# RWKV-7 recurrence on one core: TensorE work regrouped by tiling, states kept in one tile, exponentials and y transposes in other steps

## The chip, the cores and the metric

The kernel runs on one core of a Trainium2 chip. The metric is device time in microseconds (us). A core has five engines with an instruction stream each: TensorE (PE; its weight loads are listed as PEld), VectorE (DVE), ScalarE (ACT), GpSimd (POOL) and SyncE (SP), which here only issues DMAs. TensorE writes to PSUM, eight banks of 128 partitions by 512 float32; the other operands lie in SBUF. The profile's times count from the first instruction of the program.

## The reference

One inference step of a two-layer trunk: a gated DeltaNet layer and an RWKV-7 layer, on one prompt of 1024 tokens with 16 learned meta tokens ahead of it, and on 8 samples of 8 tokens. The change is in the RWKV-7 layer alone, whose core is this:

```python
def step(S, inp):
    r_t, k_t, v_t, d_t, kk_t, b_t = inp
    S = (S * d_t[:, :, None, :]
         + jnp.einsum('bhvk,bhk->bhv', S, -kk_t)[..., None] * b_t[:, :, None, :]
         + v_t[..., None] * k_t[:, :, None, :])
    return S, jnp.einsum('bhvk,bhk->bhv', S, r_t)
```

There are 16 heads with a 64x64 state each. The outputs y are normalised per head (mean, variance, weight, bias), get the bonus `sum(r*k*r_k) * v`, are gated and projected with `w_o`; the residual sum and a last RMSNorm follow.

## The kernel before

**Tiling.** The 1104 tokens are cut into three segments of 384, 384 and 336, each into six chunks of 64. Two heads form a pair, so there are 8 pairs, and one pair with one segment is an item, `P[n]`, n = 8*s + p, 24 in all. The 8 pairs' states are tiles `S[p]` of [128, 64]: the two heads' key dimensions on the partitions.

**The wave.** `wave` runs over `tau` from -3 to 54. Item n starts at `tau` = 2n and does one chunk in each step, `ci` = tau - 2n, so three items are under way at once, at chunks that lie two apart. In a step the three items' small products stand next to each other in the same PSUM banks (`pX`, `pY`, `pS`, tag "r", three banks).

**One step**, in the order of the program:
- `wave_open` takes three banks; `step_solve` multiplies the values V (the lower half of UV) with the scores G into `pX` (called "values" below), then the state S with AR into `pX` and `pY` ("solve"); ScalarE copies `pX` to X.
- `parts[0]` of the item that comes next: its scores, AR with BK, three chunks at a time into two banks of tag "f", masked to G by VectorE (L1460 to L1468).
- `step_inner`: X with TT ("TT"); ScalarE writes the negative into the upper half of UV.
- Then, each traced behind that ScalarE instruction: `step_old` (ScalarE: the old state times its decay, `pre`); steps of `rwkv_finish` for items that are done; the third part of `rwkv_front` (`pr`, its split on ScalarE, `prh`, and GpSimd); dense filling work (`fill`); `parts[1]` (the bonus in even steps; in odd ones the transposes of v, which ScalarE copies into UV at L1489).
- `step_state`: UV with BT into `pS` (state products), UV with G into `pY` (y products); VectorE makes the new states (L1600), ScalarE copies y (L1608).
- Filling work again, `parts[2]` (BK's transposes, copied to BT by ScalarE, L1476), in odd steps the y transposes of a finished item (L1645, tag "f"), `y_stats`, `rwkv_finish` up to its power on GpSimd, the loads of a new item; in even steps `front`, the second part of `rwkv_front`, with both exponentials on ScalarE (L1276, L1277), the decays' copy `DC` on GpSimd, and AR and BK on VectorE.

So an item's front goes over two steps, its parts over the next two, its six chunks over six, and its finish over three: the power, then the newton steps on VectorE (L110 to L112), `gnm` (L1636) and the y scalings on ScalarE (L1638, four in an even step, two in the odd one behind it), the transposes with `k` and `lz` on VectorE (L1647, L1648), and last the split `yh`, `yl`.

**Filling work.** `jobs` and `more` are lists of generators with a number of pieces and a first and last `tau`; `fill(now)` runs as many pieces as are due. Until `tau` 14 it is the gate projection (`zz`), then output tiles (`zo`, `do`): six dense products a piece, two pieces a tile, at whose start the next weights are cast (L86, `whi`) and at whose end VectorE adds the tile (L1740, `zst`).

**Order.** TensorE and ScalarE run in the order of the program (`manual_schedule`). VectorE, GpSimd and SyncE are ordered by a planner at build time, which takes what is ready, earlier program text first; `high_priority` puts the state update ahead. Buffers are tags with a number: a bank of "f" (two banks) is taken again as soon as its last reader is done, and the taker waits for it.

For the first segment the samples' states are read, used and written by `rwkv_sample_read` and `rwkv_sample_write`, in the first 16 steps.

Of the kernel before, what the change touches and what calls it, by code (L numbers as in the profile page):

```python
# [35 lines left out]
class Builder:  # L36
# [1368 lines left out]
    def rwkv_front(self, p, s):  # L1405
# [3 lines left out]
        P.p, P.s, P.n = p, s, 8 * s + p  # L1409
        NB = self.NB  # L1410
# [15 lines left out]
        DC = P.DC = t(fp, [128, 14], "DC", NB + 2)  # L1426
        nc.gpsimd.tensor_copy(DC[:, 0:6].unsqueeze(2), Dp[:, 1:385].rearrange("p (c k) -> p c k", k=64)[:, :, 63:64])
        if s == 0:
            nc.gpsimd.tensor_copy(DC[:, 6:14].unsqueeze(2), Dp[:, 1:65].rearrange("p (c k) -> p c k", k=8)[:, :, 7:8])
# [24 lines left out]
        def scores(c):  # L1454

            gp = [self.ps("f", 2, "G") for h in (0, 1)]
            for u in range(3):
                for h in (0, 1):
                    q = slice(64 * h, 64 * h + 64)
                    self.mm(gp[h][:, 128 * u:128 * u + 128], flat(BK[q, c + u]), AR[q, :, c + u])  # L1460
# [33 lines left out]
        if s == 0:  # L1494
            if p:
                read = self.rwkv_sample_read(P)
                next(read)
            for g in (1, 3, 5):
                P.parts[g].append(lambda: next(read, None))
        yield P  # L1500
# [36 lines left out]
    def step_solve(self, W):  # L1537

        hs = [slice(0, 64), slice(64, 128)]
        UV = self.ring_uv(W.tau)  # L1540
        for (P, ci), q in zip(W.items, W.at):
            for h in (0, 1):
                self.mmw(W, "X", h, 64 * q, P.G[:, ci, h, 0:64], UV[:, q, h])
        for (P, ci), q in zip(W.items, W.at):
# [29 lines left out]
    def step_old(self, W):  # L1574

        for P, ci in W.items:
            if 6 * P.s + ci > 1:
                P.pre = self.t(self.ap, [128, 64], "pre", 3)
                self.act(P.pre, self.S[P.p], AF.Identity, scale=P.DC[:, ci:ci + 1])

    def step_state(self, W):
# [8 lines left out]
        for (P, ci), q in zip(W.items, W.at):  # L1590
            for h in (0, 1):
                self.mmw(W, "Y", 1 - h, 64 * q, P.G[:, ci, h, 64:128], UV[:, q, h])
        with self.tc.high_priority():
            for (P, ci), q in zip(W.items, W.at):
                c = 6 * P.s + ci
                S, DC, p = self.S[P.p], P.DC, W.pS[:, 64 * q:64 * q + 64]
                if c == 1:
                    nc.vector.tensor_scalar(S, p, DC[:, ci:ci + 1], None, op0=ALU.mult)
                elif c > 1:
                    nc.vector.scalar_tensor_tensor(S, p, DC[:, ci:ci + 1], P.pre, op0=ALU.mult, op1=ALU.add)  # L1600
# [20 lines left out]
    def rwkv_finish(self, p, s, P):  # L1621
# [15 lines left out]
        for q in range(6):  # L1637
            self.act(y(q), y(q), AF.Identity, scale=rs[:, q:q + 1], bias=nm[:, q:q + 1])  # L1638
            if q == 5 or q == 3 and P.n < 23:
                yield  # L1640
        yp = self.ps("f", 2, "yT")
# [18 lines left out]
    def rwkv_sample_read(self, P):  # L1660
# [23 lines left out]
        rs = [rp, self.ps("d", 2, "rsr")]  # L1684
# [8 lines left out]
    def rwkv_sample_write(self, p, P, BT, DC):  # L1693
# [12 lines left out]
        nc.vector.tensor_tensor(P.Sb, P.Sb, DC[:, 6:14].unsqueeze(2).broadcast_to([128, 8, 64]), op=ALU.mult)  # L1706
# [219 lines left out]
    def layer1(self, ctx, right, stay, xa, xb, x):  # L1926
# [138 lines left out]
        self.S = [t(ap, [128, 64], f"rS{p}") for p in range(8)]  # L2065
# [12 lines left out]
    def wave(self, zin, first, loaded_, stay, last, pool):  # L2078
# [23 lines left out]
        def norms(s):  # L2102
            x = self.sums_in(s)
            for _ in range(2 + s):
# [3 lines left out]
        jobs = [(gates, 32, -4.5, 14), (lambda: out(0, Z), 16, 14, 22), (lambda: out(1, DD), 16, 22, 30),  # L2108
                (lambda: out(2, Z), 16, 30, 38), (lambda: out(3, DD), 16, 38, 46), (lambda: out(4, Z, None, range(6)), 12, 46, 52), (lambda: out(4, DD, x2, (6, 7)), 4, 52.1, 52.45),
                (lambda: out(5, DD, x2), 16, 52.1, 54.5), (lambda: out(6, DD, x2), 8, 54.6, 56), (lambda: self.finish_last(x2), 1, 56, 57)]  # L2110

        more = [(lambda: norms(0), 8, 31, 37.9), (lambda: norms(1), 9, 46.3, 50.2), (lambda: x2.update(self.sums_in(2, (6, 7))) or iter(()), 1, 50.3, 51),
# [33 lines left out]

        load(0)
        front()
        for tau in range(-3, 55):
            m = (tau + 2) // 2  # L2150
            parts = P[m].parts[3 * (tau % 2):3 * (tau % 2) + 3] if 0 <= m < 24 else [[], [], []]
            items = [(P[n], tau - 2 * n) for n in range(max(0, (tau - 4) // 2), min(24, tau // 2 + 1)) if 0 <= tau - 2 * n < 6]
# [79 lines left out]
```

## Time and profile before

| what | us |
|---|---|
| median of 3 runs | 2243.75 (2238.74 to 2249.12) |
| the profiled execution | 2249.0 |
| its span, first to last instruction | 2247.3 |
| the wave's first 16 steps, a stretch of | 121 (1837 to 1958) |
| its further steps | 246 (1958 to 2204) |

In the timeline a row is a start, a duration, the engine, the line, the operation, the tiles written and read, and the shapes; for a product on TensorE the pair like 64*128 is the part of the array that it uses, rows by columns, its tiling. The duration of a product includes its way through the array, so what it costs is read from start to start. A bracket tells how long the engine had been idle and what ended that. `x12` stands for twelve such instructions in a row.

### The profile page before, as it was taken

To read this page: it belongs to the slowest core of one execution; us is meant where nothing else is said; L and a number is where in the kernel's file an instruction comes from. 1 tells how busy PE (TensorE), PEld (TensorE's weight loads), DVE (VectorE), ACT (ScalarE), POOL (GpSimd) and SP (SyncE) were. 2 spreads that over 40 slices of the span, in tenths; PEclk is the share of its full clock that TensorE was granted. 3 is DMA by queue.
4 is the path that set the end of the run, shared out by engine and by line. 5 is a ranking of instruction groups with operands and counts; after the bars stand their busy time and mean duration, and the time that the engine had idled before them with its cause. 6 is when DMAs were issued, how large, how long until landed. Compare 5 with 4: busy or idle time off the path is not lost.

```text
span 2247.3 us, 55153 instructions
## 1 busy us (share of the span) xinstructions
PE 2115.6 (94%) x20452; PEld 1935.5 (86%) x20452; DVE 1551.2 (69%) x4229; ACT 1271.5 (57%) x3641; POOL 911.7 (41%) x1253
## 2 busy tenths in 40 slices
PE   5989999999999999999998999989899999999997
PEld 5888888989898898989898999979798988888876
DVE  6777858576776858577433585676887747776755
ACT  5545546555455646555633365674756446677774
POOL 3434344443434335343423154254534344444434
PEclk9999999999999999999999999989999999999999
DMA  4333242333323233343615314645566375677764
GB/s 119 94 88 106 62 113 66 101 93 92 106 73 106 64 102 95 91 115 86 187 51 152 97 52 143 223 164 177 164 183 179 109 212 158 193 222 216 228 184 144
DMA packets 430662, 292.66 MB, mean 130 GB/s; under 512 B 147145, under 2 KB 412986, under 8 KB 430394
## 3 DMA queue, kind: packets, MB, share of 16 engines
q1 hardware_dynamic: 430394, 289.14, 44.8%
q8 instruction: 161, 2.64, 0.5%
q14 instruction: 107, 0.88, 0.1%
HBM read 197.68 MB, written 91.37 MB: 129 GB/s over the span
## 4 chain that ended last, share of the span: by engine, by line
PE 57%; DVE 16%; DMA 9%; ACT 8%; issue 4%; POOL 4%; SPq 2%; DVEq 0%; POOLq 0%; ACTq 0%
PE d L76 20%; PE dz L76 5%; PE rA L76 4%; PE dk L76 4%; PE dq L76 3%; DMA attn<-drow 3%; DVE invT L473 2%; DVE invtmp L471 2%; PE rX L80 2%; DVE cvy L435 2%; PE fG L76 1%; POOL attn L545 1%; PE zo L76 1%; PE dv L76 1%; PE do L76 1%
## 5 line engine op out<-in xcount | busy, mean ns | idle before, releaser
L90 POOL TENSOR_TENSOR wlo<-wraw,whi 128x512 fp32r<-128x512 f32 (+1 forms) x246 | 324.6, 1323 | 365.4 <-ACT whi L86 329.9
L76 PE MATMUL d<-xc,whi 128*128 128x384 f32 (+2 forms) x1006 | 283.5, 341 | 0.0
L86 ACT CAST whi<-wraw 128x512 fp32r<-128x512 f32 (+1 forms) x246 | 150.2, 613 | 128.7 <-PE dq L76 50.5
L435 DVE SCALAR_TENSOR_TENSOR cvy<-raw,cw,cvy 128x408 f32<-128x408 f32 (+2 forms) x288 | 177.2, 629 | 16.6 <-ACT cvy L62 14.8
L76 PEld LDWEIGHTS d<-xc,whi 128*128 128x128 f32 (+1 forms) x1006 | 185.5, 191 | 3.1 <-DVE X L731 0.8
L76 PE MATMUL d<-xc,wlo 128*128 128x384 f32 (+3 forms) x476 | 159.0, 342 | 1.9 <-POOL wlo L90 1.9
L76 PE MATMUL dz<-xc,whi 128*128 128x384 f32 (+1 forms) x480 | 150.4, 345 | 0.0
L76 PE MATMUL d<-xa,whi 128*128 128x384 f32 (+3 forms) x450 | 144.3, 344 | 5.5 <-ACT ev L2032 3.8
L76 PE MATMUL dv<-xc,whi 128*128 128x384 f32 (+1 forms) x480 | 146.7, 335 | 0.0
L834 POOL TENSOR_SCALAR Sb<-Sb,eglb 128x128 f32<-128x128 f32 x128 | 81.5, 653 | 87.5 <-DMA Sb<-in_state_gdn 46.2
L76 PE MATMUL dz<-xa,whi 128*128 128x384 f32 (+1 forms) x288 | 101.5, 353 | 0.0
L473 DVE TENSOR_TENSOR invT<-invT,invtmp 72x31 f32<-72x31 f32 (+15 forms) x248 | 99.0, 399 | 2.8
L76 PE MATMUL dv<-xa,whi 128*128 128x384 f32 (+1 forms) x288 | 100.1, 347 | 0.1
L471 DVE TENSOR_TENSOR invtmp<-invA,invT 72x31 f32<-72x31 f32 (+15 forms) x248 | 94.3, 380 | 7.4 <-DMA invA<-ltd 4.6
L76 PEld LDWEIGHTS d<-xc,wlo 128*128 128x128 f32 (+1 forms) x476 | 90.5, 191 | 6.1 <-issue 2.7
L76 PEld LDWEIGHTS d<-xa,whi 128*128 128x128 f32 (+1 forms) x450 | 85.3, 192 | 8.7 <-ACT ev L2032 4.1
L76 PEld LDWEIGHTS dz<-xc,whi 128*128 128x128 f32 x480 | 90.3, 194 | 0.8
L76 PEld LDWEIGHTS dv<-xc,whi 128*128 128x128 f32 x480 | 88.5, 188 | 0.5 <-issue 0.4
L62 ACT ACTIVATE o<-rA,gcol 128x128 f32<-128x128 f32 x128 | 46.6, 372 | 72.7 <-DVE S L745 72.2
L62 ACT ACTIVATE attn<-attn,gcol 128x128 f32<-128x128 f32 x144 | 46.6, 390 | 72.5 <-POOL attn L545 72.4
L76 PE MATMUL d<-xa,wlo 128*128 128x384 f32 (+3 forms) x252 | 86.1, 342 | 1.4 <-POOL wlo L90 1.4
L62 ACT ACTIVATE w<-rA,nbp 128x128 f32<-128x128 f32 x144 | 51.4, 367 | 49.5 <-PE rA L76 49.0
(522 smaller groups left out, 7030.9 us busy)
## 6 DMA issues: line engine op xcount, KB each, us to landing
wraw<-in_gdn_w_in SPq DMA_DIRECT2D x96, 256.0 KB
wraw<-in_rwkv_w_rkvz SPq DMA_DIRECT2D x80, 256.0 KB
Sb<-in_state_gdn SPq DMA_DIRECT2D x64, 256.0 KB
sldcak<-cakd SPq DMA_DIRECT2D x24, 576.0 KB
wraw<-in_rwkv_w_o SPq DMA_DIRECT2D x42, 256.0 KB
E<-drow SPq DMA_DIRECT2D x24, 384.0 KB
attn<-drow SPq DMA_DIRECT2D x24, 384.0 KB
wraw<-in_gdn_w_out SPq DMA_DIRECT2D x36, 256.0 KB
```

What stands on the lines that cost most here:

```text
L62: return self.nc.scalar.activation(out, in_, func, bias=bias, scale=scale, **kw)
L76: self.nc.tensor.matmul(out, lhsT, rhs, start=start, stop=stop)
L80: self.nc.tensor.matmul(out, lhsT, rhs, start=start, stop=True, skip_group_check=True)
L86: nc.scalar.copy(hi, x)
L90: e.tensor_tensor(lo, x, hi.bitcast(F32), op=ALU.subtract)
L435: nc.vector.scalar_tensor_tensor(y[:, 0:wd], raw[:, k:k + wd], cw[k], y[:, 0:wd], op0=ALU.mult, op1=ALU.add)
L471: nc.vector.tensor_tensor(tmp, A[:, j, j + 1:32].unsqueeze(2).broadcast_to([nb, n, m]), Tv[:, j, 0:m].unsqueeze(1).broadcast_to([nb, n, m] ...
L473: nc.vector.tensor_tensor(Tv[:, j + 1:32, 0:m], Tv[:, j + 1:32, 0:m], tmp, op=ALU.subtract)
L545: nc.gpsimd.affine_select(E6, E6, pattern=[[0, 6], [1, 128]], compare_op=ALU.is_ge, fill=NEG, base=0, channel_multiplier=-1)
L834: nc.gpsimd.tensor_scalar(Sb[:, u], Sb[:, u], self.eglb[:, hv, 4 * g + u:4 * g + u + 1], None, op0=ALU.mult)
```

## The change

TensorE's work in a step is put in another order, and some other work with it:

- The values for step tau + 1 are issued at the end of step tau, right behind the y products (`step_values`, called by `opened`).
- The scores are computed with 64 columns of weights at a time instead of 128: twice as many products, half as wide.
- Both portions of filling work, `parts[1]` and `parts[2]` stand ahead of `step_state`; before, half of the filling work and `parts[2]` stood behind it.
- The y transposes come right behind `step_inner` in odd steps, into a bank of a tag chosen by `tau` (`Q.tag`). All six y scalings of an item stand in its even step.
- The second part of a front, with the exponentials, stands in odd steps behind the y transposes; the third part follows in the same step, behind the first portion of filling work.
- The 8 states lie in one tile `Sall`. `step_old` goes. The update is an addition and a multiplication on up to three neighbouring states at once, with the decays in one tile `DCr`. A segment's wrap from pair 7 to pair 0 splits it into two.
- The output tiles' due times move by 0.6, so that a tile's first piece falls into a step's second portion and its second piece into the next step's first.
- A sample's last reading step comes at the end of the odd step (`P.tail`), with its second bank from tag "f".

```diff
-        DC = P.DC = t(fp, [128, 14], "DC", NB + 2)
-        nc.gpsimd.tensor_copy(DC[:, 0:6].unsqueeze(2), Dp[:, 1:385].rearrange("p (c k) -> p c k", k=64)[:, :, 63:64])
+        nc.gpsimd.tensor_copy(self.DCr[:, 6 * p:6 * p + 6].unsqueeze(2), Dp[:, 1:385].rearrange("p (c k) -> p c k", k=64)[:, :, 63:64])
...
-                    self.mm(gp[h][:, 128 * u:128 * u + 128], flat(BK[q, c + u]), AR[q, :, c + u])
+                    for x in (0, 1):
+                        self.mm(gp[h][64 * x:64 * x + 64, 128 * u:128 * u + 128], BK[q, c + u, x], AR[q, :, c + u])
...
-    def step_solve(self, W):
-
-        hs = [slice(0, 64), slice(64, 128)]
+    def step_values(self, W):
+
         UV = self.ring_uv(W.tau)
         for (P, ci), q in zip(W.items, W.at):
             for h in (0, 1):
                 self.mmw(W, "X", h, 64 * q, P.G[:, ci, h, 0:64], UV[:, q, h])
+
+    def step_solve(self, W):
...
-    def step_old(self, W):
-
-        for P, ci in W.items:
-            if 6 * P.s + ci > 1:
-                P.pre = self.t(self.ap, [128, 64], "pre", 3)
-                self.act(P.pre, self.S[P.p], AF.Identity, scale=P.DC[:, ci:ci + 1])
...
+        live = [(P, ci, q) for (P, ci), q in zip(W.items, W.at) if 6 * P.s + ci > 0]
...
+            for r in runs:
+                (P, ci, q), n = r[0], len(r)
+                S = self.Sall[:, P.p:P.p + n]
+                x = self.t(self.ap, [128, 3, 64], "pre", 2)[:, 0:n]
+                o = 6 * P.p + ci
+                DC = self.DCr[:, o:o + 4 * n - 3:4]
+                nc.vector.tensor_tensor(x, W.pS[:, 64 * q:64 * q + 64 * n].rearrange("p (c k) -> p c k", k=64), S, op=ALU.add)
+                nc.vector.tensor_tensor(S, x, DC.unsqueeze(2).broadcast_to([128, n, 64]), op=ALU.mult)
...
             self.act(y(q), y(q), AF.Identity, scale=rs[:, q:q + 1], bias=nm[:, q:q + 1])
-            if q == 5 or q == 3 and P.n < 23:
-                yield
-        yp = self.ps("f", 2, "yT")
+        yield
+        yp = self.ps(*P.tag, "yT")
...
-        jobs = [(gates, 32, -4.5, 14), (lambda: out(0, Z), 16, 14, 22), (lambda: out(1, DD), 16, 22, 30),
+        jobs = [(gates, 32, -4.5, 14.6), (lambda: out(0, Z), 16, 14.6, 22.6), (lambda: out(1, DD), 16, 22.6, 30.6),
...
+        def opened(tau):
+            items = [(P[n], tau - 2 * n) for n in range(max(0, (tau - 4) // 2), min(24, tau // 2 + 1)) if 0 <= tau - 2 * n < 6]
+            W = self.wave_open(items, tau) if items else None
+            if W:
+                self.step_values(W)
+            return items, W
...
             with self.tc.issue_after(ins) if W else ExitStack():
-                if W:
-                    self.step_old(W)
+                if tau % 2 and 0 <= (tau - 7) // 2 < 22:
+                    Q = P[(tau - 7) // 2]
+                    Q.tag = DD if tau < 23 else Z if 23 <= tau < 30 or 39 <= tau < 46 else ("f", 2)
+                    next(Q.done)
+                if tau % 2 and loaded and tau > -2:
+                    begun.append(loaded.pop(0))
+                    next(begun[-1])
                 if tau % 2 == 0 and 0 <= (tau - 8) // 2 < 24:
                     next(P[(tau - 8) // 2].done, None)
...
                 late = [x for x in late if not next(x, True)]
+                fill(tau + 0.5)
                 for f in begun:
                     next(f)
                 begun.clear()
-                fill(tau + 0.5)
...
                 for f in parts[1]:
                     f()
-                if W:
-                    self.step_state(W)
...
                 fill(tau + 1)
                 for f in parts[2]:
                     f()
-                if tau % 2 and 0 <= (tau - 7) // 2 < 24:
-                    next(P[(tau - 7) // 2].done, None)
+                if W:
+                    self.step_state(W)
+                late = [x for x in late if not next(x, True)]
+                if tau == 51:
+                    next(P[22].done)
+                step = opened(tau + 1)
+                if tau % 2 and 0 <= m < 24 and P[m].tail:
+                    P[m].tail()
...
                 if tau % 2:
                     load((tau + 5) // 2)
-                else:
-                    front()
```

48 lines of the change are left out of this document (27 added, 21 removed).

## The prediction

> **What bounds the kernel now.** I read the page first, then the busy time by stretch, then TensorE's timeline over one pair of recurrence steps, then ScalarE's, VectorE's and GpSimd's timelines over the same pair.
>
> ```profile
> span 2247.3 us, 55153 instructions
> ...
> PE 2115.6 (94%) x20452; PEld 1935.5 (86%) x20452; DVE 1551.2 (69%) x4229; ACT 1271.5 (57%) x3641; POOL 911.7 (41%) x1253
> ```
>
> The change touches only the recurrence, some 52 steps. Its two halves (up to chunk step 16, where the samples' states are handled too, and after) by stretch; behind its length stand the busy us of PE, PEld, DVE, ACT and POOL, the granted clock, the DMA share and GB/s:
>
> ```profile
> 1837.00:1958.00 121.00, 116.92 (x1758) 96.56 (x1758) 89.82 (x296) 76.35 (x219) 54.61 (x61) 0.99 0.65 178
> 1958.00:2204.00 246.00, 236.95 (x3871) 203.73 (x3871) 167.45 (x626) 181.35 (x546) 109.31 (x118) 1.00 0.72 214
> ```
>
> The reader sees a TensorE that is never idle (237 of 246 us), at full clock, beside a ScalarE that is 74% busy. One pair on TensorE (odd step 2048.17 to 2055.62, even step to 2062.00: 13.83 us):
>
> ```profile
> 2048.17 0.57 PE L80 MATMUL rX<-UV,G 128*64 128x64 f32 x12
> ...
> 2054.78 0.91 PE L76 MATMUL fyT<-ident,y 64*64 64x64 f32 x24 [0.18 <-ACT UV L1489]
> ...
> 2055.62 0.57 PE L80 MATMUL rX<-UV,G 128*64 128x64 f32 x12
> 2056.12 0.27 PE L80 MATMUL rX<-rS,AR 64*64 64x64 f32 x2
> ...
> 2056.63 0.94 PE L76 MATMUL fG<-AR,BK 64*128 64x128 f32 x12
> 2057.49 0.27 PE L80 MATMUL rX<-X,rTT 64*64 64x64 f32 x1
> ...
> 2057.78 0.22 PE L80 MATMUL rX<-X,rTT 64*64 64x64 f32 x1
> ...
> 2057.84 0.22 PE L80 MATMUL rX<-X,rTT 64*64 64x64 f32 x1
> ...
> 2057.99 0.45 PE L76 MATMUL zo<-yh,whi 128*128 128x384 f32 x1
> 2058.27 0.34 PE L76 MATMUL zo<-yl,whi 128*128 128x384 f32 x1
> 2058.45 0.34 PE L76 MATMUL zo<-yh,wlo 128*128 128x384 f32 x1
> ...
> 2059.32 0.34 PE L76 MATMUL fbonus<-prl,bones 128*128 128x384 f32 x1
> 2059.58 0.57 PE L80 MATMUL rS<-UV,BT 128*64 128x64 f32 x12
> 2059.98 0.52 PE L80 MATMUL rY<-UV,G 128*64 128x64 f32 x12
> 2060.43 0.44 PE L76 MATMUL zo<-yh,whi 128*128 128x384 f32 x1
> ...
> 2062.00 0.57 PE L80 MATMUL rX<-UV,G 128*64 128x64 f32 x12
> ```
>
> The tiling stands behind the operands. Inside a group a round starts 0.06 us after the last (2057.78, 2057.84); where the tiling changes it takes 0.15 (2057.84 to 2057.99), and a first dense product then holds 0.28 instead of 0.18 (2057.99, 2058.27, 2058.45). A change costs 0.09, into a dense piece 0.19. After a dense product it is the same 0.09 (2059.32 to 2059.58, 0.26 instead of 0.17).
>
> **The change, part by part.**
>
> *Regrouping.* Before, the tiling changes 8 times in an odd step and 7 in an even one; afterwards three times in each (64*64, then 128*128, then 128*64). Nine changes fewer at 0.09, and two entries of four into dense work at another 0.10: 1.0 us a pair. The y transposes also lose their 0.18 of waiting. TensorE alone would need 13.83 - 1.2 = 12.6.
>
> *Scores as 24 products of 64 columns instead of 12 of 128.* No such row exists. The solve puts 24 products of 64*64 into 0.51 us (2056.12 to 2056.63), four tiles at once, with half the moving columns; doubling the columns gives up to 1.0, and equal streaming (two row halves now, four tiles then, over the same columns) 0.75 without the change of tiling. I take 0.75, since now two tiles are at work in 0.86 (2056.63 to 2057.49) and the four do the same total. The Trainium skill speaks against it ("TensorE: Matmul & The Clock Gate", section "Wait — 56ns, not 53.3ns?"): starts never come closer than about 25 ns, and 62 ns each where hardware decode is off. By 25 ns the sum stays; by 62 ns the scores would take an estimated 1.5 us. The solve's 24 in 0.51 us disagree with both.
>
> *State update.* Three fused operations and three ScalarE products (`pre`) become two operations on 128x192. For the rest of this part ScalarE and VectorE:
>
> ```profile
> 2052.61 0.50 ACT L86 CAST prh<-pr 128x384 fp32r<-128x384 f32 x1
> ...
> 2053.65 1.07 ACT L1489 COPY UV<-fVT 64x128 f32<-64x128 f32 x4
> 2054.75 0.32 ACT L1608 COPY y<-rY 128x192 f32<-128x192 f32 x1
> 2054.96 0.48 ACT L1476 COPY BT<-fBT 128x384 f32<-128x384 f32 x1
> ...
> 2058.09 0.33 ACT L62 ACTIVATE UV<-rX 64x192 f32<-64x192 f32 x1 [1.04 <-PE rS L80]
> 2058.32 0.31 ACT L62 ACTIVATE UV<-rS 64x192 f32<-64x192 f32 x1
> 2058.66 0.83 ACT L62 ACTIVATE pre<-rS,DC 128x64 f32<-128x64 f32 x3
> ...
> 2059.80 1.43 ACT L62 ACTIVATE y<-y,gnm,grs 128x64 f32<-128x64 f32 x4
> 2061.13 0.60 ACT L86 CAST whi<-wraw 128x512 fp32r<-128x512 f32 x1
> ```
>
> ```profile
> 2049.46 0.56 DVE L1431 TENSOR_TENSOR AR<-fldrv,fDp 128x384 f32<-128x384 f32 x1 [0.35 <-DMA fldrv<-rvd]
> 2049.94 0.55 DVE L1434 TENSOR_TENSOR BK<-fld2c,fiD 128x384 f32<-128x384 f32 x1
> 2050.41 0.61 DVE L1441 SCALAR_TENSOR_TENSOR pr<-fldrv,pcol,fld2c 128x384 f32<-128x384 f32 x1
> ...
> 2054.31 0.55 DVE L1740 TENSOR_TENSOR zst<-zst,do 128x384 f32<-128x384 f32 x1 [0.85 <-PE do L76]
> ...
> 2055.77 0.61 DVE L1647 SCALAR_TENSOR_TENSOR k<-fyT,lnw,rbv 128x384 f32<-128x384 f32 x1
> 2055.94 1.32 POOL L102 TENSOR_TENSOR grs<-va,cvals 128x6 f32<-128x6 f32 x1 [0.52 <-DVE va L1631]
> 2057.90 0.17 DVE L1636 SCALAR_TENSOR_TENSOR gnm<-mv,grs 128x6 f32<-128x6 f32 x1
> 2057.98 1.01 DVE L1467 TENSOR_TENSOR G<-fG,gm 128x384 f32<-128x384 f32 x2
> 2060.28 0.67 DVE L1600 SCALAR_TENSOR_TENSOR rS<-rS,DC,pre 128x64 f32<-128x64 f32 x3
> ```
>
> ```profile
> L62 ACT ACTIVATE fDp<-fld2c 128x384 f32<-128x384 f32 x23 | 12.3, 537 | 0.0
> ...
> L1465 DVE TENSOR_TENSOR G<-fG,gms 128x128 f32<-128x128 f32 x14 | 4.0, 285 | 1.5 <-PE fG L76 1.5
> ```
>
> 128x192 lies between 0.285 (128x128) and 0.55 (128x384): 0.35 each, as a guess from those ends. ScalarE is relieved of 3 x 0.24 a step, which is worth nothing by itself. What is new is that little covers the update: it starts 0.70 after the state products (2059.58 to 2060.28), ends at 0.70 + 0.35 + 0.35, and reaches TensorE at 1.5, which by then has had the state products 0.40, the y products 0.35 and the next step's values 0.45, 1.2 in all. TensorE waits 0.3 a step with the whole next step behind it. Bound by TensorE alone, a pair takes 12.6 + 0.6 = 13.2.
>
> *Exponentials, y scaling and transposes moved; this decides.* ScalarE runs in the order of the program. In an odd step the exponentials now stand behind UV, and `prh` right behind them; `prh` needs `pr`, hence AR and BK, hence the exponentials. Before, half a step lay between. Let T be the first product with TT, 1.16 after the solve (0.41 + 0.75). UV starts T+0.60 and ends T+1.14 (2057.49, 2058.09, 2058.63); two exponentials at 0.54, overlapping by 0.1, end at T+2.1. VectorE gets k at T+1.3 (24 transposes behind the TT products) and has k 0.61, lz 0.62, AR 0.56, BK 0.55, zst 0.55 ahead of `pr`, if it takes what is ready in program order, 0.05 overlapped each: `pr` runs T+4.1 to T+4.75, and ScalarE has stood still from T+2.1 to T+4.8. Behind it wait the UV copies of the new item, the weight cast, BT, and the copy of y. The values need the first half of the copies: T+4.8, cast 0.4, half of 1.07, the last four products and a change 0.25: the next solve at T+6.0. The odd step takes 1.16 + 6.0 = 7.2 (now 7.45). ScalarE goes on: copies to T+6.3, cast 0.5, BT to T+7.3.
>
> The even step E begins at T+6.0. Its scores need the PSUM bank that BT empties at E+1.3, instead of E+0.41; TT follows 0.75 later, at 2.1; then 0.50, two dense pieces 1.15 + 1.05, bonus 0.35, keys 0.42, 0.40 + 0.35 + 0.45 and the 0.3 of waiting: 7.0 (now 6.38). The copy of y starts at E+1.3 too; from there to gnm it is 3.3 (2054.75 to 2058.07, GpSimd's power 1.32 in it), so the y scalings, now six at 0.335 (1.43 for four, overlapping), run E+4.6 to E+6.7, cast and BT end at E+7.65, and the next scores wait again, 0.3. The pair takes 7.0 + 7.2 + 0.3 = 14.5 against 13.83, 0.6 more.
>
> From 1958 to 2204 lie 17.8 pairs: +11 to +12 us. In the first 16 steps ScalarE is less full (76 of 121 us) and VectorE fuller (90 of 121); I take 0 there, with -0.6 and +0.6 a pair as ends (5 us either way).
>
> *The rest.* The cleared state tile and the decay copies are small and lie on VectorE and GpSimd beside other work; the decay copy is queued behind the exponential as before. Front's moved step issues no DMA; SP keeps its order but for a tile's loads, half a step later. GpSimd's part of `pr` ends a microsecond behind `prh`, long before the bonus needs it. If any becomes late it costs its 0.3 to 0.5 once a pair, inside the range.
>
> The profiled execution took 2249.0, 5 over the median 2243.75; +12 on either gives 2261 and **2256**.
>
> **Rivals.**
>
> *A, faster: the new order on ScalarE does not bind.* If VectorE does AR, BK and `pr` as soon as the exponentials are there, `prh` starts at T+3.4, 1.4 earlier, BT is out in time, and a pair falls to TensorE's 13.2 or 13.3: -0.5 x 17.8 = -9, with the early half -14: 2230, ends 2222 and 2236. For it: the planner, not the program, orders VectorE, and TensorE is what binds today. Against: k and lz come earlier in the program and are ready first.
>
> *B, no change.* AR and BK between k and lz, `pr` before zst: 0.5 off my sum, a pair of 14.0: +3, 2247.
>
> *C, slower by more.* VectorE's row at 2057.90 shows the power's successors ahead of the G masks. Kept so, the masks would hold both score banks until E+4.5, the bonus and all behind it waits: above 15 a pair, +1.2 x 17.8 = +21, 2265. It decides from the point where the power ends later than the scores, which the late copy of y brings.
>
> *D, slower: products cost per instruction.* If a score product keeps its 0.063 (0.76 over 12), 24 take 1.5, 0.75 more in each step: 1.5 x 17.8 on top of my sum, 2283 and beyond. The solve speaks against it. The 62 ns of the Trainium skill ("TensorE: Matmul & The Clock Gate", as above) would act like this.
>
> **How the numbers follow.** My case 0.34, A 0.33, B 0.16, C 0.14, D 0.03. My case spans 2249 to 2262 (0.3 to 0.9 a pair). A change of under 0.5% (11 us) can't be told from none here. My case splits 0.24 slower, 0.10 within; with C and D slower is 0.41; A gives 0.32 faster; the rest, 0.27, is within. The range leaves out A's lowest fifth, C's top and D: 2224 to 2272.
>
> **What would show it.** Right: a wait of `prh` for `pr` of about 2.5 us in each odd step on ScalarE; `y` waiting for gnm in even ones; the first score product waiting for BT; pairs near 14.5; TensorE's busy share falling below 93% in the late half. A is right if `prh` waits under 1.5 and pairs are near 13.2, with a wait of about 0.3 for the state. Wrong in all cases would be score groups above 1 us, or a state update above 0.9.

## The result and the profile after

| kernel | median, us | ratio to before | 95% interval |
|---|---|---|---|
| before | 2242.22 | 1 | |
| after | 2299.19 | 1.0253 | 1.0222 to 1.0283 |

The kernel is slower by 57 us, where 12 were forecast: the direction was right, the size far off, and the time lies above the range of 2224 to 2272. The profiled execution of after has a span of 2298.6 us, 51.3 over that of before. The page of after, its first line and its busy times:

```profile
span 2298.6 us, 56108 instructions
...
PE 2102.3 (91%) x21028; PEld 1935.5 (84%) x21028; DVE 1576.7 (69%) x4212; ACT 1245.7 (54%) x3513; POOL 921.6 (40%) x1253
```

The same two stretches as shown of before (length, busy us of PE, PEld, DVE, ACT and POOL, the granted clock, the DMA share, GB/s):

```profile
1837.00:1958.00 121.00, 102.03 (x1691) 88.64 (x1690) 82.83 (x255) 64.32 (x173) 52.25 (x55) 0.90 0.53 148
1958.00:2204.00 246.00, 201.30 (x3774) 178.19 (x3772) 161.61 (x527) 139.56 (x382) 98.52 (x105) 0.97 0.64 188
```

TensorE is busy for 201 of 246 us (237 before), and no other engine is fuller: it has become a chain of waits between engines. The clock has fallen as well, to 0.90 in the early stretch (0.99 before).

To add it up, I went through the timeline from the values of step 0 to those of step 51 in windows of 2 us: TensorE's idle time is the window less its busy time, the clock's loss is the busy time times one less the granted clock, and the rest is work at full clock.

| us | before | after | difference |
|---|---|---|---|
| steps 0 to 16 | 122.4 | 142.8 | +20.4 |
| steps 16 to 51 | 244.6 | 284.5 | +39.9 |
| in both: TensorE idle | 13.1 | 76.7 | +63.6 |
| lost to a lower clock | 1.7 | 23.6 | +21.9 |
| work at full clock | 352.2 | 327.0 | -25.2 |

These steps take 60.3 us longer, more than the whole program, because the part ahead of them was 8 us shorter in this execution; the values of step 0 lie anywhere from 1823.7 to 1843.8 in the kernels shown here.

TensorE's work falls as it should: 25 us less in 25.5 pairs, 0.99 a pair. The narrower scores are in that; alone, in the kernel before, they take 12.3 us off. The added waits are two and a half times the saving, and the lower clock costs nearly as much as was saved. Who ends TensorE's waits in the late steps (us in total, times, longest):

```profile
PE rX L80 <- DVE rS L1607: 18.2, 30, 3.3
PE zo L76 <- DVE zst L1746: 13.0, 13, 1.7
PE fsT L73 <- DVE G L1469: 7.6, 3, 2.5
PE dfin L73 <- DVE f2k L1782: 5.7, 1, 5.7
PE fbonus L76 <- DVE G L1469: 3.0, 3, 1.4
PE rX L80 <- ACT X L1564: 2.5, 5, 1.0
PE fyT L76 <- DVE G L1469: 2.4, 4, 1.6
PE fG L76 <- ACT BT L1478: 1.9, 4, 0.7
```

These eight are 54.3 of the 55.5 us that TensorE stands idle there, and 49.9 of them end with VectorE. ScalarE, on which the forecast rested, ends 4.4. That a wait ends with VectorE doesn't make VectorE its cause, since VectorE stands too: over all these steps 26.2 us in its first newton step for GpSimd's power, and 13.4 in AR for the exponentials on ScalarE. TensorE's timeline over one pair:

```profile
1988.24 0.52 PE L80 MATMUL rX<-UV,G 128*64 128x64 f32 x12
1989.08 0.27 PE L80 MATMUL rX<-rS,AR 64*64 64x64 f32 x2 [0.32 <-DVE rS L1607]
...
1989.49 0.84 PE L76 MATMUL fG<-AR,BK 64*64 64x128 f32 x24
...
1992.24 0.34 PE L76 MATMUL fbonus<-prl,bones 128*128 128x384 f32 x1
1993.67 0.44 PE L76 MATMUL zo<-yh,whi 128*128 128x384 f32 x1 [1.09 <-DVE zst L1746]
...
1997.24 0.27 PE L80 MATMUL rX<-rS,AR 64*64 64x64 f32 x2 [0.73 <-DVE rS L1607]
...
2000.70 0.49 PE L73 MATMUL fVT<-ident,fldrv 128*128 128x128 f32 x3
2002.67 0.44 PE L76 MATMUL zo<-yh,whi 128*128 128x384 f32 x1 [1.49 <-DVE zst L1746]
...
2004.99 0.52 PE L80 MATMUL rX<-UV,G 128*64 128x64 f32 x12
```

The pair takes 16.75 us (1988.24 to 2004.99), 3.63 of it in the four brackets. What is left, 13.1, is TensorE's own time. The two largest brackets are the first product of an output tile, and they wait for the addition of the tile before. VectorE in the even step, then over the odd one:

```profile
1991.27 0.17 DVE L110 TENSOR_TENSOR gn_t<-grs 128x6 f32<-128x6 f32 x1 [1.43 <-POOL grs L102]
...
1993.06 0.55 DVE L1746 TENSOR_TENSOR zst<-zst,zo 128x384 f32<-128x384 f32 x1
...
2000.07 0.56 DVE L1432 TENSOR_TENSOR AR<-fldrv,fDp 128x384 f32<-128x384 f32 x1 [0.45 <-ACT fDp L62]
2000.54 0.61 DVE L1653 SCALAR_TENSOR_TENSOR k<-dyT,lnw,rbv 128x384 f32<-128x384 f32 x1
2001.07 0.55 DVE L1435 TENSOR_TENSOR BK<-fld2c,fiD 128x384 f32<-128x384 f32 x1
2001.54 0.61 DVE L1442 SCALAR_TENSOR_TENSOR pr<-fldrv,pcol,fld2c 128x384 f32<-128x384 f32 x1
2002.07 0.55 DVE L1746 TENSOR_TENSOR zst<-zst,zo 128x384 f32<-128x384 f32 x1
```

In the odd step the tile is complete on TensorE at about 2000.70. Its addition stands in VectorE's queue behind AR, `k`, BK and `pr`, runs at 2002.07, and only then is the one bank of tag "z" free. In the even step the addition stands behind the masks and the newton steps, for the first of which VectorE had stood still for 1.43 us. Before, a tile ended with the second portion of filling work, and the next began a whole solve later. Now, with due times 0.6 later and both portions ahead of `step_state`, one tile ends with a step's first portion, and the next begins with its second, with only the bonus or v's transposes between. With two banks (tag "d") the next tile needn't wait: out(1)'s pairs took 13.6 to 14.6.

The wait for the state, 18.2 us in 30 times, has three parts. In 13 of them it is 0.15 to 0.34 us, 3.1 in all, as forecast. Twice VectorE comes to the update late, which costs 3.1 and 3.3 us. The other 15 times, 8.6 us in all, the second operation of the update takes 0.48 to 1.18 us, where it otherwise takes 0.36 at most, and each time GpSimd is at work on `wlo` or `prl`:

```profile
2012.80 1.27 POOL L90 TENSOR_TENSOR wlo<-wraw,whi 128x512 fp32r<-128x512 f32 x1 [2.94 <-ACT whi L86]
2012.89 0.36 DVE L1606 TENSOR_TENSOR pre<-rS,rS 128x192 f32<-128x192 f32 x1 [1.86 <-PE rS L80]
2013.28 1.00 DVE L1607 TENSOR_TENSOR rS<-pre,DCr 128x192 f32<-128x192 f32 x1
2014.34 0.27 PE L80 MATMUL rX<-rS,AR 64*64 64x64 f32 x2 [0.86 <-DVE rS L1607]
```

The first operation, which reads a product in PSUM, isn't held up; the second, which reads two tensors in SBUF, ends just behind GpSimd's piece.

The early steps show the clock. TensorE, then VectorE ahead of its wait, then the windows around it (same columns as above):

```profile
1902.66 0.49 PE L73 MATMUL fVT<-ident,fldrv 128*128 128x128 f32 x3
1905.44 0.65 PE L76 MATMUL zz<-xa,whi 128*128 128x336 f32 x1 [2.29 <-DVE zst L1003]
```

```profile
1902.71 0.55 DVE L1435 TENSOR_TENSOR BK<-fld2c,fiD 128x384 f32<-128x384 f32 x1
1903.18 0.61 DVE L1442 SCALAR_TENSOR_TENSOR pr<-fldrv,pcol,fld2c 128x384 f32<-128x384 f32 x1
1903.71 0.61 DVE L1653 SCALAR_TENSOR_TENSOR k<-dyT,lnw,rbv 128x384 f32<-128x384 f32 x1
1904.36 0.62 DVE L1654 SCALAR_TENSOR_TENSOR lz<-k,lnb,lz 128x384 f32<-128x384 f32 x1
1904.89 0.50 DVE L1003 SCALAR_TENSOR_TENSOR zst<-zst,zz 128x336 f32<-128x336 f32 x1
```

```profile
1904.00:1906.00 2.00, 0.56 (x2) 0.56 (x3) 1.35 (x3) 1.76 (x4) 1.51 (x2) 0.83 0.79 236
1906.00:1908.00 2.00, 2.00 (x9) 1.67 (x7) 0.00 (x0) 0.00 (x0) 1.14 (x1) 0.50 0.84 208
```

It is the same collision, on the gate projection's tiles: BK, `pr`, `k` and `lz` stand ahead of the addition. TensorE idles for 2.29 us and afterwards works at half its clock for some 3 us. The clock is halved nine times in the first 16 steps, once before the change. Only three of the nine follow a tile that waits for an addition. Five follow scores that wait for `xss`, the copies of the samples' products, which since the change hold a bank of tag "f" (9.3 us in 7 times):

```profile
1857.52 1.33 PE L76 MATMUL fG<-AR,BK 64*64 64x128 f32 x18 [1.77 <-DVE xss L1697]
```

### The profile page after: what moved, and what is told of

Read it like the earlier page. It is cut to its first block, busy times and chain, and to the rows that moved or that the text cites. A ratio compares the mean times of both kernels' runs of the same rounds, so it can differ in the third digit from the quotient of the medians.

```text
span 2298.6 us, 56108 instructions
## 1 busy us (share of the span) xinstructions
PE 2102.3 (91%) x21028; PEld 1935.5 (84%) x21028; DVE 1576.7 (69%) x4212; ACT 1245.7 (54%) x3513; POOL 921.6 (40%) x1253
## 5 line engine op out<-in xcount | busy, mean ns | idle before, releaser
L435 DVE SCALAR_TENSOR_TENSOR cvy<-raw,cw,cvy 128x408 f32<-128x408 f32 (+2 forms) x288 | 177.8, 630 | 16.5 <-ACT cvy L62 14.7
L76 PE MATMUL d<-xa,whi 128*128 128x384 f32 (+3 forms) x450 | 142.8, 341 | 5.7 <-ACT ev L2038 4.0
L834 POOL TENSOR_SCALAR Sb<-Sb,eglb 128x128 f32<-128x128 f32 x128 | 81.2, 651 | 89.4 <-DMA Sb<-in_state_gdn 49.9
```

Of the source, the lines that this page charges most:

```text
L76: self.nc.tensor.matmul(out, lhsT, rhs, start=start, stop=stop)
L435: nc.vector.scalar_tensor_tensor(y[:, 0:wd], raw[:, k:k + wd], cw[k], y[:, 0:wd], op0=ALU.mult, op1=ALU.add)
L834: nc.gpsimd.tensor_scalar(Sb[:, u], Sb[:, u], self.eglb[:, hv, 4 * g + u:4 * g + u + 1], None, op0=ALU.mult)
```

## The experiments

Times differ by some us from one set to the next, so kernels are compared by their ratio to the kernel before, run beside them. 0.001 is 2.2 us. Theories: T1, tiles collide since the due times moved; T2, ScalarE's order, as forecast; T3, the state update has lost its cover; T4 and T5 come up further down.

| what is undone or added | median | ratio | interval |
|---|---|---|---|
| after, old due times | 2278.31 | 1.0128 | 1.0087 to 1.0170 |
| after, samples' bank back | 2298.63 | 1.0228 | 1.0183 to 1.0272 |
| after, exponentials back | 2283.08 | 1.0147 | 1.0108 to 1.0186 |
| after, `prh` later in the odd step | 2292.11 | 1.0216 | 1.0185 to 1.0247 |
| after, state update ahead of the 2nd portion | 2274.41 | 1.0131 | 1.0103 to 1.0159 |
| after, old due times, exponentials back | 2264.27 | 1.0095 | 1.0067 to 1.0122 |
| after, these and the state update | 2246.85 | 1.0017 | 0.9996 to 1.0039 |
| the same, loads behind stores | 2241.85 | 0.9990 | 0.9969 to 1.0010 |
| before, later due times | 2259.57 | 1.0049 | 1.0027 to 1.0072 |
| before, scores 64*64 | 2239.46 | 0.9989 | 0.9970 to 1.0008 |
| before, states in one tile | 2243.39 | 0.9994 | 0.9975 to 1.0013 |
| before, loads behind stores | 2241.96 | 0.9991 | 0.9973 to 1.0009 |
| before, scores 64*64, loads behind stores | 2235.24 | 0.9955 | 0.9938 to 0.9971 |
| before, these and states in one tile | 2233.93 | 0.9954 | 0.9933 to 0.9974 |

The stretch from the values of step 0 to those of step 51, split as above, in one profiled execution of each (us):

| kernel | stretch | TensorE idle | lost to the clock | work |
|---|---|---|---|---|
| before | 367.0 | 13.1 | 1.7 | 352.2 |
| after | 427.3 | 76.7 | 23.6 | 327.0 |
| after, old due times | 404.4 | 64.0 | 13.1 | 327.4 |
| after, exponentials back | 410.4 | 74.2 | 8.7 | 327.5 |
| after, `prh` later in the odd step | 408.9 | 69.2 | 14.5 | 325.2 |
| after, old due times, exponentials back | 389.4 | 51.0 | 10.9 | 327.5 |
| after, state update ahead of the 2nd portion | 402.2 | 43.9 | 17.0 | 341.2 |
| after, all three | 372.0 | 30.0 | 5.4 | 336.6 |

### The due times

```diff
-        jobs = [(gates, 32, -4.5, 14.6), (lambda: out(0, Z), 16, 14.6, 22.6), (lambda: out(1, DD), 16, 22.6, 30.6),
...
+        jobs = [(gates, 32, -4.5, 14), (lambda: out(0, Z), 16, 14, 22), (lambda: out(1, DD), 16, 22, 30),
```

and so for all of them, in after:

> The changed kernel with the old due times for the output tiles and the norms (14, 22, 30, 38, 46 and so on, 0.6 earlier than the change has them); nothing else differs. Theory T1 (collision of tiles): shifted by 0.6, the last piece of one tile and the first of the next stand in the same step, and with one PSUM bank (tag z) the next tile waits for VectorE's addition to zst; 15.2 us of TensorE's waits in the trace of the changed kernel stand behind zst of the output tiles and some 10 more behind work that this pushes late. T1 expects 2270 to 2284, pairs of some 14 us where they are 17 now (out(0)), and no wait of zo for zst. Theory T2 (the prediction's: ScalarE stands at prh for pr, y for gnm): within 5 us of 2299, pairs as now. Theory T3 (the state update has lost its cover and VectorE is late with it): within 5 us of 2299, the 21.1 us of rX waiting for rS stay.

The ratio falls from 1.0253 to 1.0128, and no wait of `zo` for `zst` is left among the larger ones: T1 holds. But pairs are 15.0 to 15.3, not 14, in out(0) and out(1) alike. What holds them now is in the main what the forecast had described. TensorE in the odd step, and ScalarE ahead of it:

```profile
2015.49 0.34 PE L80 MATMUL rX<-UV,G 128*64 128x64 f32 x4 [0.76 <-ACT UV L1491]
```

```profile
2014.43 0.51 ACT L86 CAST prh<-pr 128x384 fp32r<-128x384 f32 x1 [2.30 <-DVE pr L1442]
```

`prh` waits 2.3 us for `pr`, UV is copied late behind it, and the values of the next step wait. Of these 2.3 us the forecast's sum lacks one: `pr` takes 1.64 us from 2012.70 on instead of 0.61, with GpSimd at `wlo` from 2012.20 to 2013.92. In after, the collision may have hidden this by being later still; that is argued, not shown. The mirror image, the later due times in the kernel before:

> The kernel before with the due times alone shifted by 0.6 as in the change. T1: the collision of tiles costs there too: 2253 to 2270, with zo waiting for zst. T2 and T3: 2238 to 2248, no difference.

It costs 0.5%, but hardly through a wait for `zst` (`zo` waits 2.3 us in two times): there the state and y products stand between the portions. What it does cost by is open. The shift alone isn't the collision; it takes the other edit too, `step_state` behind both portions.

### The exponentials

`next(begun[-1])` goes from the start of the odd step back to the end of the even one (`else: front()`), in after:

> The changed kernel with the exponentials, AR and BK issued at the end of the even step as before, half a step ahead of pr and prh; nothing else differs. T2 (ScalarE's order decides): prh no longer waits for pr (30.5 us in 20 waits now), and the time falls by 20 or more, to 2260 to 2280. T1 and T3: prh's wait goes too, but TensorE stood behind VectorE and not behind ScalarE, so the time falls by 8 at most, 2291 to 2299.

The ratio falls to 1.0147, within T2's time. Yet it is hardly the waiting that goes: TensorE idles for 74.2 us instead of 76.7. The clock's loss falls from 23.6 to 8.7, and most of that in the first 16 steps (15.2 to 1.7). There the gaps add up to 21 us as before, but three instead of nine last 1.3 us or more. To tell `prh` from AR and BK, another run leaves the exponentials where the change puts them and moves only `pr`, `prh`, `prl` and the load of TT to the end of the odd step:

```diff
-                for f in begun:
-                    next(f)
-                begun.clear()
                 if tau == 52:
...
                 step = opened(tau + 1)
+                for f in begun:
+                    next(f)
+                begun.clear()
```

> The changed kernel with the exponentials where the change puts them (start of the odd step), but pr, prh, prl and the load of TT moved from the middle to the end of that odd step, behind the copies of UV, BT and y. T2 in the prediction's form (ScalarE stands at prh, and UV, the cast, BT and y behind it): as much as moving the exponentials back gave (-16), 2280 to 2288. If instead VectorE's AR and BK in the odd step are what costs: 2294 to 2302.

1.0216: 0.4% less, and the intervals of the two kernels overlap; it lies between the two expectations. The total doesn't settle it, though. In the table above this kernel needs 408.9 us from step 0 to step 51, no more than with the exponentials back. It loses ahead of that: from the first AR to step 0 it takes 19.4 us (14.7 in after, 12.6 with the exponentials back), and the first AR itself came 4.6 us later than with the exponentials back. So within the steps moving `prh` alone gave as much, although AR and BK stayed in VectorE's queue of the odd step, and `zo` waited 20.3 us for `zst`, more than in after. How much of the loss is ScalarE's stand at `prh` and how much is VectorE's queue stays open.

Both undone together:

> The changed kernel with two things undone together: the old due times, and the exponentials with AR and BK at the end of the even step. Alone they gave -21 (2278) and -16 (2283). T1 and T2 as separate causes: the gains add to 2262, or more, since with the old due times prh's wait for pr had grown to 45.2 us and late UV showed at TensorE (7.0 us). One cause with two names: 2275 to 2283. T3 (the state update without cover) expects rX to keep waiting for rS for 15 to 25 us in either case.

0.0158 less than after, where the two alone give 0.0125 and 0.0106; with these intervals that can hardly be told from a sum. The median, 2264, is what was expected of two separate causes, and in the table the stretch is 37.9 us shorter, where the two alone make it 22.9 and 16.9 shorter. So they are two causes in the main. In the first 16 steps nothing is left of the loss (122.2 us, no window under 0.8 clock).

### The samples' bank

> The changed kernel with the second product tile of the samples' read (rsr) in the tag d as before, instead of the tag f that the scores use; nothing else differs. T1 in its wider form (banks handed out differently): the 9.3 us of scores waiting for xss in the first 16 steps go, 2286 to 2293. T2 and T3: within 4 us of 2299, since neither has to do with that bank; the time would come back as another wait of the first 16 steps.

No difference, so T1's wider form falls: the scores' wait for `xss` went, and a wait of `drsr` for `Sb`, 9.1 us, took its place. VectorE is late with the samples' work in either bank.

### The place of the state update

```diff
+                if W:
+                    self.step_state(W)
                 fill(tau + 1)
                 for f in parts[2]:
                     f()
-                if W:
-                    self.step_state(W)
```

> The changed kernel with the state and y products, and with them the state update, back ahead of the step's second fill (after the bonus) as before; the values of the next step stay where the change has them. T3 (the second fill was the update's cover, and also what stood between two tiles' products): rX's wait for rS, 21.1 us, falls to 5 or less and zo's wait for zst, 15.2 us, to 5 or less: 2262 to 2275. T1 in its first form (the due times alone make the collision): zo's wait stays at 10 or more and only rS's goes, 2275 to 2285. T2: both waits come back as waits for UV and BT, 2290 or more.

TensorE's waits of this kernel:

```profile
PE fbonus L76 <- DVE G L1469: 10.1, 9, 3.0
...
PE zo L76 <- DVE zst L1746: 4.9, 7, 1.2
...
PE rX L80 <- DVE rS L1607: 1.5, 5, 0.6
```

T3: the wait for the state falls from 21.1 to 1.5, the one for `zst` from 15.2 to 4.9, and the ratio to 1.0131. The second portion was the cover of the update and the distance between two tiles at once. GpSimd still holds up the update's second operation (up to 1.10 us), but the wait for it is small.

### All three, and what the rest is worth

> The changed kernel with three things of order undone together: old due times, exponentials at the end of the even step, state update ahead of the second fill. What is left of the change: scores as 64*64 products, one tile of states with two operations, values ahead of the step's end, y transposes behind the TT products, banks. If order is the whole loss, what is left gains: the state's wait gone too, TensorE alone needs some 13 us a pair, 2215 to 2240. If one of the parts left costs (banks, y transposes, the scores' form), 2250 to 2265.

1.0017, as before the change: these three explain the loss. But what is left of the change, 0.9 us in an undisturbed pair, gains nothing. Not all of the regrouping is left: the state and y products stand between the two portions again, and TensorE's work is 9.6 us more than in after. A pair without disturbance:

```profile
2015.53 0.57 PE L80 MATMUL rX<-UV,G 128*64 128x64 f32 x12
2022.40 0.57 PE L80 MATMUL rX<-UV,G 128*64 128x64 f32 x12
2028.44 0.57 PE L80 MATMUL rX<-UV,G 128*64 128x64 f32 x12
```

That is 6.87 + 6.04 = 12.9. Others take 15 to 20. VectorE, and the windows of one of these:

```profile
2063.35 0.56 DVE L1432 TENSOR_TENSOR AR<-fldrv,fDp 128x384 f32<-128x384 f32 x1 [3.11 <-DMA fldrv<-rvd]
```

```profile
2064.00:2068.00 4.00, 1.56 (x25) 1.45 (x25) 2.85 (x4) 0.51 (x1) 2.43 (x3) 0.50 0.43 129
2068.00:2072.00 4.00, 4.00 (x36) 3.63 (x37) 1.87 (x4) 1.20 (x3) 0.00 (x0) 0.69 0.83 243
```

VectorE's queue stands at AR until a load has landed, the G masks behind it, the scores' banks with them; `pr`, between them, takes 1.62 us instead of 0.61, again with GpSimd at `wlo`. TensorE idles for 4.9 us and gets half the clock. One suspect was SyncE, whose queue stands at the next tile's load of `zst` until an earlier store has landed. So the load was ordered behind the store of the tile before it (T4):

```diff
+                with self.tc.issue_after(stored) if stored else ExitStack():
                     nc.sync.dma_start(x[:, 0:n], self.x1T[ft][:, c0:c0 + n])
...
-                nc.sync.dma_start(self.x1T[ft][:, c0:c0 + n], x[:, 0:n])
+                stored = nc.sync.dma_start(self.x1T[ft][:, c0:c0 + n], x[:, 0:n]).ins
```

> The kernel with the three things of order undone (due times, exponentials, state update ahead of the second fill; 2247 us), and beside that each output tile's load of zst ordered behind the store of the tile before it. In the trace of that kernel pairs take 12.9 us, but some stand still: VectorE waits for the load of fldrv (13.2 us in 6 times), TensorE behind it, and the clock granted then is 0.5 for some 4 us. SyncE's queue stands at the load of the next tile's zst until a store has landed (up to 6.4 us), and later loads with it. Theory T4 (what the rest of the change gains is taken back by these late loads): AR's wait for fldrv falls to 4 or less in all, and the time to 2225 to 2238. Rival T5 (the loads are late because the transfers themselves are slow, or something else holds the pairs): 2243 to 2252.

AR's wait falls from 13.2 to 1.8 us, but now `zst` waits 5.8 for its load, pairs of 19.0 and 15.7 remain, and the intervals overlap: the wait went from one load to another. As a control in the kernel before:

> The kernel before with the order of loads and stores alone, a control. It has 6.9 us of AR waiting for fldrv in 5 times. T4: these go, 2232 to 2240. T5: 2240 to 2248; with the loads of zst now later, VectorE could wait for them instead (zst waiting for its load).

No difference that can be told. Single parts in the kernel before:

> The kernel before with the scores alone as 24 products of 64 columns on 64*64. In the changed kernel 24 of them take 0.66 us to the next group, against 0.94 for the 12 of before, and two changes of tiling (0.09 each) go as well: some 0.4 a step in 48 steps, 2222 to 2232 on 2245. If it is priced by the instruction (the prediction's rival D): 24 at 0.063, 0.6 a step more, 2265 to 2275. If a step is bound elsewhere (the chain through ScalarE), no change, 2240 to 2248.

Undisturbed pairs fall from 13.8 to 13.2, and the time hardly moves: in this trace AR waits once 2.9 us for its load, TensorE idles 2.45, and a pair takes 18.5. With the loads behind the stores:

> The kernel before with the scores as 64*64 products (2239 us, pairs of 13.15 with two long ones of 18.5 and 16.5) and the same order of loads and stores. T4: the two long pairs become ordinary: 2228 to 2235. T5: 2235 to 2243.

0.9955, faster by less than half a per cent. The pair of 18.5 is gone, one of 16.3 is left, and the time lies at the edge of both ranges, so T4 isn't decided by it. The states in one tile alone, at the update's old place:

> The kernel before with the states in one tile and updated by two operations for three items, at its old place, so without the ScalarE products pre. If the new form of the update is harmless and only its place cost (T3): 2236 to 2246, no wait of rX for rS above 3 us in all. If the form itself costs (two operations in a chain, 0.7 instead of 0.67): 2248 or more with rX waiting for rS.

At its old place, where other products cover it, the form of the update is harmless, though GpSimd holds up its second operation here too (up to 1.33 us). Added to the two before:

> The kernel before with the scores as 64*64 products, the order of loads and stores (together 2235), and the states in one tile at the update's old place. If ScalarE's relief (three products pre a step) is worth something once TensorE needs less: 2225 to 2232; if TensorE alone binds (pairs of 13.2): 2232 to 2240.

0.9954: the best of these, faster than both kernels, but the update adds nothing that shows.

### More slack for the load

If late loads of `fldrv` are the trouble, the change's own place for AR has half a step more. With the old due times, the update ahead of the second portion, and `prh` at the end of the odd step:

> The changed kernel with the old due times, the state update ahead of the second fill, and pr and prh at the end of the odd step; the exponentials stay at its start, so that AR has the load of fldrv half a step later than in the kernel with all three things undone (2247 us). T4 (late loads of fldrv took the gain back): AR's wait for fldrv is 2 or less in all, no pair stands still up to step 30, pairs of 13.0 to 13.3: 2225 to 2238. T5 (another cause): pairs that stand still with other waits, 2242 to 2252.

2297.75 (1.0245, 1.0221 to 1.0270), a clear miss: pairs of 17.2. VectorE and GpSimd in an even step:

```profile
2027.52 1.01 POOL L90 TENSOR_TENSOR prl<-pr,prh 128x384 fp32r<-128x384 f32 x1
2027.58 0.97 DVE L110 TENSOR_TENSOR gn_t<-grs 128x6 f32<-128x6 f32 x1 [1.43 <-POOL grs L102]
2028.49 0.99 POOL L90 TENSOR_TENSOR yl<-lz,yh 128x384 fp32r<-128x384 f32 x1
2028.58 0.92 DVE L111 SCALAR_TENSOR_TENSOR gn_t<-gn_t,va 128x6 f32<-128x6 f32 x1
...
2029.82 1.02 DVE L1469 TENSOR_TENSOR G<-fG,gm 128x384 f32<-128x384 f32 x2
```

This is the prediction's rival C: the planner put the power's successors ahead of the masks, and VectorE stands from 2026.1 to 2027.6 for GpSimd, with both score banks held. Two of the four successors then take 0.97 and 0.92 us instead of 0.17, next to GpSimd's `prl` and `yl`, which holds the masks up by another 1.55 us. The bonus waits 17.8 us in all. With the samples' write and bank put back as well it is the same (2301.36; 1.0252, 1.0219 to 1.0285):

> As the kernel before it in this set, and the samples' read with its second bank in tag d and its last stage with keys(3), and the samples' write ahead of the second fill, all three as before the change. The scores' wait for xss (5 to 9 us in the first 16 steps) goes: 4 to 8 less than the other, 2220 to 2232; if the bank only hands the wait on to another product (as when the bank alone was put back), the same as the other.

Then only that order was changed, `newton()` and `gnm` behind the last mask:

> The kernel with the old due times, the state update ahead of the second fill and pr and prh at the end of the odd step (2298 us, pairs of 17.2), and beside that the three successors of GpSimd's power on VectorE ordered behind the step's G masks. Rival C of the prediction, as an order in VectorE's queue: the bonus's wait for G (17.8 us in 9 records, 2.1 at most) goes, a pair falls by 2 to 3, to 14 to 15, and the time to 2240 to 2262. If the order isn't the cause (the waits come back as other waits for VectorE): 2285 to 2300.

2280.00 (1.0166, 1.0134 to 1.0198). The bonus's wait is gone and pairs are 14.5 to 15, as expected of C; the total is less of a gain than expected (143.9 us in the first 16 steps). What binds now, TensorE's and ScalarE's largest waits:

```profile
PE fG L76 <- ACT BT L1478: 21.4, 20, 3.3
```

```profile
ACT y L62 <- DVE gnm L1644: 36.1, 20, 2.7
```

The y scalings wait for `gnm`, BT's copy stands behind them on ScalarE, and the next scores wait for its bank: the chain that the forecast had described for the even step, at about the length it gave a pair, 14.5.

**Open** stays why a load lands late in some pairs once pairs are near 13 us, and what the rest of the change would gain without that.

## Why the prediction was wrong

- *Regrouping, 1.0 + 0.18 a pair:* right in size. Work fell by 0.99 a pair, the narrower scores with it; in the late steps it is 12.6 a pair, as given for TensorE alone.
- *Scores at 0.75:* right, a little long: 0.67 from 1989.49 to the first TT product at 1990.16. Rival D, priced by the instruction, is out.
- *State update, two operations of 0.35, TensorE waiting 0.3 a step:* right where nothing disturbs it (0.36 each, a wait of 0.15 to 0.34). Overall the term was too small, 18.2 us over the 35 late steps, 0.52 a step. Beside GpSimd's `wlo` and `prl` the second operation takes up to 1.18 us, and the update then lasts over 0.9, which the forecast had named as a sign of being wrong. With the update in its old place some 27 us went (0.0122 of 2242), more than the wait itself, because the place also kept the tiles apart.
- *"This decides", ScalarE's order:* the waits are there as forecast (`prh` for `pr` up to 2.6 us, 32.4 in 21 times; `y` for `gnm`; TensorE's share at 82% late), but they end only 4.4 of TensorE's 54.3 us of waits directly. Moving `prh` away gave 0.4% in all, with 18 us between steps 0 and 51, so ScalarE's share isn't settled. The chain is seen to bind, at 15 and 14.6 us a pair, when the other waits are taken away (old due times; masks first). So the sum for a pair was not bad for a kernel that isn't this one. In that sum the terms given put `pr` at T+3.9 rather than T+4.1, which changes little.
- *"The rest", where "if any becomes late it costs its 0.3 to 0.5 once a pair":* **the step that failed.** Of a tile's pieces it was said only that its loads come half a step later. That the next tile's first product now stands right behind the last one's, with one bank between, was overlooked. It cost 2.58 a pair in the pair shown (1.09 + 1.49), five times the bound, and undoing the due times gave back 0.0125. The trace of before had the pieces: `zst` needs 0.55 on VectorE, and in the odd step operations of 0.55 to 0.61 were about to be put ahead of it. The forecast's own sum had `zst` ahead of `pr`. VectorE took `pr` first, the order of rival B, which was priced as a gain of 0.5 because the wait of the next tile was not in it.
- *The first 16 steps, taken as 0 with 5 us either way:* +20.4. TensorE idles 17 us more there and loses 13.5 more to the clock, behind the samples' `xss` above all and behind the gate projection's tiles.
- *Not in the sum at all:* what an idle TensorE costs afterwards. 21.9 us of lost clock come on top of 63.6 of waiting, a third more.
- *The direction,* slower, came out right in part by luck: the waits that were to decide it are a small part of those that TensorE shows.
- *Rivals:* C was given 0.14 and a price of 15 a pair. Its start is there in after, VectorE standing 1.43 us for the power at 1991.27, but the masks run between the power's successors. With `prh` at the end of the odd step it is there in full, at 17.2.

## What to carry to other kernels

Where a change moves dense filler, follow each of its tiles from the last product through the addition that frees its bank to the next tile's first product, with everything that stands in the adding engine's queue meanwhile; one bank and two products next to each other are a wait. Work that covers one dependence often keeps two others apart, so ask of every move what it stood between. Price TensorE's idle time with what the clock adds behind it. And where VectorE's work is on the critical path, look at what GpSimd does meanwhile: an operation that read two tensors in SBUF was held up by it, one that read PSUM was not.

## What the hardware showed unexpectedly

- Gaps of about 2 us can halve the granted clock. In the first 16 steps of after, gaps of 1.77 us (1855.75 to 1857.52) and 2.29 us (1903.15 to 1905.44) were each followed by half the clock for 3.4 us. Not every gap does it: one of 2.55 us (2169.92 to 2172.47) was followed by none. The Trainium skill ("TensorE: Matmul & The Clock Gate", section "HAM oscillation — how this bites in real kernels") gives gaps over some 3.4 us as the ones to avoid; half the clock agrees, the length of the gap doesn't: shorter ones did it here.
- Products of 64*64 on four tiles start far closer together than 25 ns: 24 of the solve took 0.41 us (1989.08 to 1989.49), 17 ns each. The Trainium skill ("TensorE: Matmul & The Clock Gate", section "Wait — 56ns, not 53.3ns?") gives about 25 ns as the least distance of two starts; taken over all four tiles the trace disagrees, while on one tile six products in 0.41 us are 68 ns apart.
- VectorE's operations that read two tensors in SBUF were held up by GpSimd's `wlo`, `prl` and `yl`. In after, 21 of the 24 second operations of the update that began beside one of these took longer, up to 1.18 us, and none of the 35 others did (0.36 at most). The first operation, which reads PSUM, took no longer in any of 30 such cases, and neither did the fused update of before in 77 (0.27 to 0.29). The statistics of y (`bnst`), which read one tensor in SBUF, took 0.21 to 0.23 us in 45. The newton steps show the same as the update: 0.97 and 0.92 instead of 0.17 (2027.58 and 2028.58 above).
